# A prefix log-sum-exp kernel: TensorE's unrolled products become a loop in a loop, and semaphores are set by hand

## The chip, the cores and the metric

The kernel runs on one core of one Trainium2 chip. The metric is the device time of one execution in microseconds (us), as the median of several runs. Lower is better.

## The reference

For each of 4 batches, a running log-sum-exp is taken along 4096 rows, separately in each of 4128 columns. Input and output are float32, 270.5 MB each.

```python
B, S, D = (4, 4096, 4128)
out[:, 0, :] = x[:, 0, :]
for t in range(1, S):
    mx = np.maximum(out[:, t - 1, :], x[:, t, :])
    out[:, t, :] = mx + np.log(np.exp(out[:, t - 1, :] - mx) + np.exp(x[:, t, :] - mx))
```

## The kernel before

The fast path `_fast` computes log(prefix sum of exp(x)). It also gathers a few sums and lowest values into a flag. If the flag says that the plain exponentials were out of range, a slow path `_general` does the work again; with this input it is not taken.

**Tiles.** The work is cut into 44 steps, 11 for each batch. A step holds 384 rows (`R` = 3: each of 128 partitions holds three consecutive rows), or 256 rows in one step of each batch (the first of batch 0, the last of the others). A step is loaded by one DMA of 6192 KB (4128 KB for the short ones) and stored by one DMA of the same size from the same tile `xt`. There are `BUFS` = 4 such tiles in turn. SyncE issues all loads and stores in an order written out by hand: the store of step k when its four logarithms are done, then the load of step k + 3, which goes into the tile of step k - 1 and waits until the store of that step has landed.

**Chunks.** The 4128 columns of a step are worked on in four chunks: three of 1024 columns, with a running base `base0` to `base2` in PSUM, and one of 1056, whose base is in `carry` in SBUF. For each chunk ScalarE takes the exponential (L115), VectorE adds up the rows inside each partition (`sums`, L119), TensorE multiplies with the triangle `excl` to get what lies in the partitions above (`head`, L126; `head_rest`, L134 and L136, for the last chunk, 512 columns at a time through `q`), VectorE adds this base to the rows (`add`, L150; `add_rest`, L143; `keep`, L155, for the last chunk), TensorE passes the last row on with `pick` (`pass_on`, L159), and ScalarE takes the logarithm (L171). GpSimd copies the first row of each batch for the flag (L197), and VectorE reduces these copies and the last bases (L202, L166).

**Order.** Each engine has a list of steps, in an order given by the tables `ORDER`, `DORDER`, `PORDER` and some for the first and last steps. A loop emits from the lists whatever has its needs met, and the framework sets the semaphores between engines from the tiles that each instruction reads and writes. All engines are fully unrolled; on TensorE, all 781 products stand one after another in the program. A float32 product shows as two weight loads and two matmuls in the trace.

Of the kernel before, what the change touches and what calls it, by code (L numbers as in the profile page):

```python
# [6 lines left out]

# [5 lines left out]
P = 128  # L13
# [10 lines left out]
SPLIT = False  # L24
# [5 lines left out]
def _constants(nc, pool):  # L30

    def triangle(base, name):
        t = pool.tile([P, P], FP32, name=name)
        nc.gpsimd.memset(t, 1.0)
        nc.gpsimd.affine_select(
            out=t, in_=t, pattern=[[1, P]], compare_op=ALU.is_ge,
            fill=0.0, base=base, channel_multiplier=-1,
        )
        return t

    excl = triangle(-1, "excl")
    pick = pool.tile([P, P], FP32, name="pick")
    nc.gpsimd.memset(pick, 0.0)
    nc.gpsimd.affine_select(
        out=pick, in_=pick, pattern=[[0, P]], compare_op=ALU.not_equal,
        fill=1.0, base=-(P - 1), channel_multiplier=1,
    )
    ones = pool.tile([P, 1], FP32, name="ones")
    nc.gpsimd.memset(ones, 1.0)
    return excl, pick, ones  # L50


def _fast(ctx, tc, x, out, flag):

# [9 lines left out]
    excl, pick, ones = _constants(nc, consts)  # L64
    xpool = ctx.enter_context(tc.tile_pool(name="xpool", bufs=BUFS))
    cpool = ctx.enter_context(tc.tile_pool(name="cpool", bufs=1))
    pkeep = ctx.enter_context(tc.tile_pool(name="pkeep", bufs=1, space=bass.MemoryType.PSUM))
    prest = ctx.enter_context(tc.tile_pool(name="prest", bufs=2, space=bass.MemoryType.PSUM))

    carry = cpool.tile([P, rest], FP32, name="carry")  # L70
    first = cpool.tile([1, D], mybir.dt.bfloat16, name="first")
    low = cpool.tile([1, 1], FP32, name="low")
    part = cpool.tile([P, 5 * B], FP32, name="part")
    every = cpool.tile([P, 1], FP32, name="every")
    nc.vector.memset(carry, 0.0)  # L75
    nc.vector.memset(part, 0.0)
    base = [pkeep.tile([P, CH], FP32, name=f"base{c}") for c in range(3)]

    ctx.enter_context(tc.manual_schedule())

    class Step:
        def __init__(self, b, row, r):
            self.b, self.row, self.r = b, row, r
            self.first = row == 0
            self.last = row + P * r == S

# [4 lines left out]
        def load(self):  # L91
            full = xpool.tile([P, R, D], FP32, name="xt")
            self.xt = full[:, :self.r, :]
            nc.sync.dma_start(out=self.xt, in_=self.dram(x))

        def store(self, lo=0, hi=D):
            nc.sync.dma_start(out=self.dram(out)[:, :, lo:hi], in_=self.xt[:, :, lo:hi])

    class Chunk:
        def __init__(self, step, c):  # L100
            self.t, self.c = step, c
            self.a = c * CH
            self.w = CH if c < 3 else rest
            self.end = c == 3
            self.q = {}
# [7 lines left out]
        def exp(self):  # L113
            rows = self.rows(0, self.t.r)
            nc.scalar.activation(rows, rows, ACT.Exp)  # L115

        def sums(self):
            for j in range(1, self.t.r):
                nc.vector.tensor_tensor(  # L119
                    out=self.row(j), in0=self.row(j - 1), in1=self.row(j), op=ALU.add)  # L120

        def head(self):
            t = self.t
            own = self.row(t.r - 1)
            for s in range(0, CH, MM):
                nc.tensor.matmul(base[self.c][:, s:s + MM], lhsT=excl, rhs=own[:, s:s + MM],  # L126
                                 start=t.first, stop=True, skip_group_check=True)

        def head_rest(self, i):
            t = self.t  # L130
            s, w = subs[i]
            q = self.q[i] = prest.tile([P, MM], FP32, name="q")
            if not t.first:
                nc.tensor.matmul(q[:, :w], lhsT=pick, rhs=carry[:, s:s + w],  # L134
                                 start=True, stop=False, skip_group_check=True)
            nc.tensor.matmul(q[:, :w], lhsT=excl, rhs=self.row(t.r - 1)[:, s:s + w],  # L136
                             start=t.first, stop=True, skip_group_check=True)

        def add_rest(self, i):
            t = self.t  # L140
            s, w = subs[i]
            rows = t.xt[:, :, self.a + s:self.a + s + w]
            nc.vector.tensor_tensor(  # L143
                out=rows, in0=rows, in1=self.q[i][:, :w].unsqueeze(1).to_broadcast([P, t.r, w]),
                op=ALU.add)

        def add(self):
            t = self.t
            rows = self.rows(0, t.r)
            nc.vector.tensor_tensor(  # L150
# [3 lines left out]
        def keep(self):  # L154
            nc.vector.tensor_copy(carry[HI:P, :], self.row(self.t.r - 1)[HI:P])  # L155

        def pass_on(self):
            for s in range(0, CH, MM):
                nc.tensor.matmul(base[self.c][:, s:s + MM], lhsT=pick,  # L159
                                 rhs=self.row(self.t.r - 1)[:, s:s + MM],  # L160
                                 start=True, stop=False, skip_group_check=True)

        def total(self):
            own = carry if self.end else base[self.c]
            i = 4 * self.t.b + self.c
            nc.vector.tensor_reduce(  # L166
                out=part[HI:P, i:i + 1], in_=own[HI:P, :self.w], axis=AX.X, op=ALU.add)

        def ln(self):
            rows = self.rows(0, self.t.r)  # L170
            nc.scalar.activation(rows, rows, ACT.Ln)  # L171

    steps = []
    for b in range(B):
# [5 lines left out]
        for r in parts:  # L180
            steps.append(Step(b, row, r))
            row += P * r
# [3 lines left out]
    T = len(steps)  # L186
    heads = [k for k in range(T) if steps[k].first]
    done = set()
    act, dve, pe, pool, sync = [], [], [], [], []

    def put(queue, name, work, *needs):
        queue.append((name, work, needs))

    def lowest(t, c):

        a, w = c * CH, CH if c < 3 else rest
        nc.gpsimd.tensor_copy(first[:, a:a + w], t.xt[0:1, 0, a:a + w])  # L197

    def lower(t):

        i = 4 * B + t.b
        nc.vector.tensor_reduce(out=low, in_=first, axis=AX.X, op=ALU.min)  # L202
        nc.vector.tensor_scalar(
            out=part[0:1, i:i + 1], in0=low, scalar1=1.0 / LIMIT, scalar2=2 * LIMIT, op0=ALU.is_lt, op1=ALU.mult)

    for k, t in enumerate(steps):
        C = chunks[4 * k:4 * k + 4]
        prev = chunks[4 * k - 4:4 * k] if k else []
        W = len(subs)

        def exp(c):
            put(act, ("exp", k, c), C[c].exp, ("load", k))

        def ln(kk, c):
            put(act, ("ln", kk, c), chunks[4 * kk + c].ln, ("keep" if c == 3 else "pass", kk, c),
                *[("low", kk, c)] * steps[kk].first)

        order = {0: FIRST, T - 2: LATE, T - 1: LAST}.get(k, ORDER)
        for o in order:
            if o[0] == "e":  # L220
                exp(int(o[1]))
            elif o[0] == "n":
                put(act, ("exp", k + 1, int(o[1])), chunks[4 * k + 4 + int(o[1])].exp, ("load", k + 1))
# [4 lines left out]
        if t.first:  # L228
            for c in range(4):
                put(pool, ("low", k, c), lambda t=t, c=c: lowest(t, c), ("exp", k, c),  # L230
                    *[("lower", j) for j in heads if j < k])

        def sums(c):
            put(dve, ("sums", k, c), C[c].sums, ("exp", k, c))

        def add(c):
            put(dve, ("add", k, c), C[c].add, ("head", k, c))

        for o in DORDER:
            if o[0] == "s":  # L240
                sums(int(o[1]))
            elif o[0] == "a":
                add(int(o[1]))
            else:
                for i in range(W):
                    put(dve, ("rest", k, i), lambda i=i, C=C: C[3].add_rest(i), ("headr", k, i))
        put(dve, ("keep", k, 3), C[3].keep)
        for j in heads:
            if k == j + min(4, heads[1] - 1):
                put(dve, ("lower", j), lambda j=j: lower(steps[j]), *[("low", j, c) for c in range(4)])  # L250
        if t.last and k < T - 1:
            for c in range(4):
                put(dve, ("total", k, c), C[c].total, ("keep" if c == 3 else "pass", k, c))

        def head(c):
            put(pe, ("head", k, c), C[c].head, ("sums", k, c), ("total", k - 1, c) if k and steps[k - 1].last else ("sums", k, c))

        def headr(i):
            put(pe, ("headr", k, i), lambda C=C: C[3].head_rest(i), ("sums", k, 3),
                ("keep", k - 1, 3) if k else ("sums", k, 3), ("rest", k, i - 2) if i >= 2 else ("sums", k, 3))  # L260

        def onward(c):
            put(pe, ("pass", k, c), C[c].pass_on, ("add", k, c))

        for o in PORDER:
            if o[0] == "h":
                head(int(o[1]))
            elif o[0] == "p":
                onward(int(o[1]))
            else:  # L270
                headr(int(o[1]))

        if k < BUFS:
            put(sync, ("load", k), t.load)
    for c in range(4):
        if any(o == f"p{c}" for o in LAST) and not any(o == f"l{c}" for o in LAST):
            put(act, ("ln", T - 1, c), chunks[-4 + c].ln, ("keep" if c == 3 else "pass", T - 1, c))
    for k, t in enumerate(steps):
        if k < T - 1:
            put(sync, ("store", k), t.store, *[("ln", k, c) for c in range(4)])  # L280
# [112 lines left out]
```

## Time and profile before

| | |
|---|---|
| median of 3 runs | 1263.26 us (1262.83 to 1263.33) |
| profiled execution, own time | 1263.05 us |
| its span, first to last instruction | 1261.3 us |
| DMA moved | 541.40 MB, mean 429 GB/s |
| share of the span in which packets of the data queue (q1) were under way, over 16 DMA engines | 99.5% |
| busy: PE / DVE / ACT / POOL | 61% / 84% / 73% / 2% |
| instruction queues: q8 / q14 | 13 packets, 0.21 MB / 14 packets, 0.11 MB |

The span is measured inside the profiled execution; 1.75 us of its own time lie outside the span. PE is TensorE, DVE is VectorE, ACT is ScalarE, POOL is GpSimd, SP is SyncE, which issues the DMAs. "Share" is of the span. Queues q8 and q14 carry the program's instructions to the engines; they use the same 16 DMA engines as the data.

### The profile page before, as it was taken

How to read it: one execution, taken by the hardware profiler on the slowest of the kernel's cores; microseconds unless marked ns; L12 is line 12 of the kernel's file. 1: busy time of each engine (PE TensorE's matmuls, PEld its weight loads, DVE VectorE, ACT ScalarE, POOL GpSimd, SP SyncE). 2: the span in 40 equal slices, each digit the busy share in tenths (PEclk: the TensorE clock that was granted, in tenths of full speed). 3: DMA queues.
4: the chain of work that ended last, by engine and by line, in shares of the span. 5: the costliest groups of instructions: out<-in, count | busy, mean ns of one | idle time of the engine just before them, and what ended most of it. 6: DMA issues, size and time to landing. Idle time of an engine off the chain costs nothing.

```text
span 1261.3 us, 4886 instructions
## 1 busy us (share of the span) xinstructions
PE 767.4 (61%) x1562; PEld 308.9 (24%) x1562; DVE 1053.9 (84%) x672; ACT 925.6 (73%) x353; POOL 26.2 (2%) x25
## 2 busy tenths in 40 slices
PE   4667665565655556655566666665556666665564
PEld 1222222222222222222222222222222222222221
DVE  4999997889878898888789889888878988988785
ACT  4987777777777777768579767766866877766792
POOL 2000000000100000000010000000010000000000
PEclk9898888888888888888788888888877888888887
DMA  9999999999999999999999999999999999999998
GB/s 411 411 442 430 429 429 434 437 430 426 435 432 431 429 440 428 434 430 433 434 433 438 431 432 429 438 430 433 433 432 433 434 434 436 430 432 434 430 419 352
DMA packets 12699, 541.40 MB, mean 429 GB/s; under 512 B 1408, under 2 KB 1408, under 8 KB 1408
## 3 DMA queue, kind: packets, MB, share of 16 engines
q1 hardware_dynamic: 12672, 541.07, 99.5%
q8 instruction: 13, 0.21, 0.1%
q14 instruction: 14, 0.11, 0.0%
HBM read 270.53 MB, written 270.53 MB: 429 GB/s over the span
## 4 chain that ended last, share of the span: by engine, by line
DMA 55%; DVE 22%; ACT 12%; issue 5%; PE 5%; ACTq 0%; SPq 0%; DVEq 0%
DMA xt<-in_x_dram 31%; DMA out_dram<-xt 24%; DVE xt L150 10%; ACT xt L171 6%; DVE xt L119 6%; ACT xt L115 6%; PE base L126 4%; DVE xt L143 3%; DVE part L166 1%; PE base L159 1%; DVE carry L155 1%; DVE low L202 0%; PE q L136 0%; PE q L134 0%; ACTq L171 0%
## 5 line engine op out<-in xcount | busy, mean ns | idle before, releaser
L115 ACT ACTIVATE xt<-xt 128x3072 f32<-128x3072 f32 (+3 forms) x176 | 465.4, 2692 | 187.3 <-DMA xt<-in_x_dram 187.3
L126 PE MATMUL base<-xt,excl 128*128 128x512 f32 x528 | 348.4, 813 | 364.1 <-DVE xt L119 324.7
L171 ACT ACTIVATE xt<-xt 128x3072 f32<-128x3072 f32 (+3 forms) x176 | 470.1, 2695 | 133.4 <-PE base L159 133.1
L119 DVE TENSOR_TENSOR xt<-xt 128x1024 f32<-128x1024 f32 (+1 forms) x336 | 417.4, 1246 | 129.9 <-ACT xt L115 124.0
L150 DVE TENSOR_TENSOR xt<-xt,base 128x3072 f32<-128x3072 f32 (+1 forms) x132 | 429.3, 3252 | 56.8 <-PE base L126 56.8
L159 PE MATMUL base<-xt,pick 128*128 128x512 f32 x528 | 260.9, 617 | 110.6 <-DVE xt L150 110.6
L126 PEld LDWEIGHTS base<-xt,excl 128*128 128x128 f32 x528 | 131.7, 265 | 546.2 <-issue 467.4
L159 PEld LDWEIGHTS base<-xt,pick 128*128 128x128 f32 x528 | 90.2, 189 | 282.1 <-DVE xt L150 216.9
L143 DVE TENSOR_TENSOR xt<-xt,q 128x1536 f32<-128x1536 f32 (+1 forms) x132 | 153.6, 1214 | 6.1 <-PE q L136 6.0
L136 PE MATMUL q<-xt,excl 128*128 128x512 f32 (+1 forms) x264 | 106.2, 486 | 1.7 <-DVE xt L119 1.7
L134 PE MATMUL q<-carry,pick 128*128 128x512 f32 (+1 forms) x240 | 93.9, 473 | 0.0
L134 PEld LDWEIGHTS q<-carry,pick 128*128 128x128 f32 x240 | 44.5, 189 | 58.5 <-issue 30.1
L136 PEld LDWEIGHTS q<-xt,excl 128*128 128x128 f32 x264 | 45.6, 190 | 47.9 <-issue 46.4
L197 POOL CAST first<-xt 1x1024 bf16<-1x1024 f32 (+1 forms) x16 | 25.1, 1574 | 927.0 <-ACT xt L115 927.0
L155 DVE COPY carry<-xt 32x1056 f32<-32x1056 f32 x44 | 31.1, 706 | 1.5
L202 DVE TENSOR_REDUCE low<-first 1x1 f32<-1x4128 bf16 x4 | 17.8, 4440 | 0.1
L166 DVE TENSOR_REDUCE part<-base 32x1 f32<-32x1024 f32 x12 | 14.1, 1223 | 0.1
L166 DVE TENSOR_REDUCE part<-carry 32x1 f32<-32x1056 f32 x4 | 5.0, 1238 | 0.0
L311 PE MATMUL q<-ones,every 128*1 128x1 f32 x2 | 0.2, 163 | 6.1 <-DVE every L309 6.1
L354 ACT ACT_TABLE_LOAD x1 | 1.3, 1283 | 0.8 <-PEq L377 0.8
L75 DVE MEMSET carry<- 128x1056 f32 x1 | 0.9, 938 | 1.1 <-PEq L377 1.1
L311 PEld LDWEIGHTS q<-ones,every 128*1 128x1 f32 x2 | 0.1, 80 | 6.1 <-issue 6.1
(13 smaller groups left out, 2.5 us busy)
## 6 DMA issues: line engine op xcount, KB each, us to landing
xt<-in_x_dram SPq DMA_DIRECT2D x40, 6192.0 KB, 43.8
out_dram<-xt SPq DMA_DIRECT2D x40, 6192.0 KB, 33.0
xt<-in_x_dram SPq DMA_DIRECT2D x4, 4128.0 KB, 31.7
out_dram<-xt SPq DMA_DIRECT2D x4, 4128.0 KB, 29.5
```

Source lines behind the costliest of these rows:

```text
L115: nc.scalar.activation(rows, rows, ACT.Exp)
L119: nc.vector.tensor_tensor(out=self.row(j), in0=self.row(j - 1), in1=self.row(j), op=ALU.add)
L126: nc.tensor.matmul(base[self.c][:, s:s + MM], lhsT=excl, rhs=own[:, s:s + MM], start=t.first, stop=True, skip_group_check=True)
L134: nc.tensor.matmul(q[:, :w], lhsT=pick, rhs=carry[:, s:s + w], start=True, stop=False, skip_group_check=True)
L136: nc.tensor.matmul(q[:, :w], lhsT=excl, rhs=self.row(t.r - 1)[:, s:s + w], start=t.first, stop=True, skip_group_check=True)
L143: nc.vector.tensor_tensor(out=rows, in0=rows, in1=self.q[i][:, :w].unsqueeze(1).to_broadcast([P, t.r, w]), op=ALU.add)
L150: nc.vector.tensor_tensor(out=rows, in0=rows, in1=base[self.c].unsqueeze(1).to_broadcast([P, t.r, CH]), op=ALU.add)
L155: nc.vector.tensor_copy(carry[HI:P, :], self.row(self.t.r - 1)[HI:P])
L159: nc.tensor.matmul(base[self.c][:, s:s + MM], lhsT=pick, rhs=self.row(self.t.r - 1)[:, s:s + MM], start=True, stop=False, skip_group_check ...
L166: nc.vector.tensor_reduce(out=part[HI:P, i:i + 1], in_=own[HI:P, :self.w], axis=AX.X, op=ALU.add)
L171: nc.scalar.activation(rows, rows, ACT.Ln)
L197: nc.gpsimd.tensor_copy(first[:, a:a + w], t.xt[0:1, 0, a:a + w])
```

## The change

TensorE's products are no longer unrolled. An outer loop runs over the batches and an inner loop over the steps of a batch; the first step of a batch stands in the outer loop by itself, because its products start new sums. The tile of a step is reached through a register, which holds the byte offset of one of four slots in a single SBUF tensor `xs`. A step of 256 rows now lies at the end of its slot, so that its last row is where that of the others is. The loop is placed so that its first instruction is the first of a block of instructions that is fetched together (`head_slot`).

Because the framework cannot follow tiles through such a register, all waits are written by hand, in one critical section for all engines. VectorE raises a semaphore `turn` after each group of sums, each `add` and the first `add_rest`; TensorE waits until it is at least 1 and takes 1 off, before eight of its nine groups of products of a step. The other engines count on one semaphore each, and each of the four slots has one semaphore for its loads and one for its stores. The other engines stay unrolled, and the orders of all engines, the tile sizes, the operations and the DMAs are those of before. In the built program ScalarE has 410 instructions and waits in place of 607, VectorE 733 in place of 783, SyncE 269 in place of 241; TensorE has 34 products in place of 781.

```diff
-        def head(c):
-            put(pe, ("head", k, c), C[c].head, ("sums", k, c), ("total", k - 1, c) if k and steps[k - 1].last else ("sums", k, c))
...
+AWAITED = {"h0", "h1", "p0", "h2", "p1", "r0", "p2", "r2"}
...
+class Line:
...
+    def wait(self, sem, value):
+        if self.seen.get(sem.num, 0) < value:
+            self.engine.wait_ge(sem, value)
+            self.seen[sem.num] = value
...
+    raw = consts.tile([P, 4 * BUFS * R * D], mybir.dt.uint8, name="xs")
+    xs = raw.bitcast(FP32).rearrange("p (s j d) -> p s j d", s=BUFS, j=R)
...
+            self.xt = xs[:, k % BUFS, R - r:R, :]
...
         def sums(self):
             for j in range(1, self.t.r):
-                nc.vector.tensor_tensor(
+                if j > 1:
+                    dve.ended += 1
+                    end.then_inc(dve.sem, 1)
+                    dve.wait(dve.sem, dve.ended)
+                end = nc.vector.tensor_tensor(
                     out=self.row(j), in0=self.row(j - 1), in1=self.row(j), op=ALU.add)
...
+    def emit(line):
+        for name, work, needs in line.steps:
+            for sem, value in sorted({ends[n] for n in needs}, key=lambda e: e[1]):
+                line.wait(sem, value)
+            end = work()
+            if line is sync:
+                sem = (landed if name[0] == "load" else stored)[name[1] % BUFS]
+                ends[name] = (sem, 16 * (name[1] // BUFS + 1))
+                end.then_inc(sem, 16)
+            elif name[0] in turns or name[0] == "rest" and name[2] == 0:
+                end.then_inc(sems["turn"], 1)
+            else:
+                line.ended += 1
+                ends[name] = (line.sem, line.ended)
+                end.then_inc(line.sem, 1)
...
+    def product(o, t, new):
+        c = int(o[1])
+        def own(a, w):
+            return raw[:, bass.ds(t + 4 * ((R - 1) * D + a), 4 * w)].bitcast(FP32)
...
+        if o in AWAITED:
+            nc.tensor.sem_inc(sems["turn"], -1).wait_op(sems["turn"], 1, "sem-ge")
+        for ps, lhsT, rhs, start, stop in work:
+            end = nc.tensor.matmul(ps, lhsT=lhsT, rhs=rhs, start=start, stop=stop, skip_group_check=True)
+        end.then_inc(sems["pe"], 1)
+
+    def tile_of(t, new):
+        slot = nc.tensor.snap((t % BUFS) * (4 * R * D))
         for o in PORDER:
-            if o[0] == "h":
-                head(int(o[1]))
-            elif o[0] == "p":
-                onward(int(o[1]))
-            else:
-                headr(int(o[1]))
...
+            product(o, slot, new)
+
+    with tc.tile_critical():
+        _constants(nc, pool, excl, pick, ones)
+        nc.tensor.wait_ge(pool.sem, pool.ended)
...
+        emit(dve)
+        emit(act)
+        emit(pool)
+        emit(sync)
+        pe = mybir.EngineType.PE
+        with nc.Fori(0, T, N, engines=OrderedEngineSet([pe]), head_slot={pe: 0}) as b:
+            tile_of(b, True)
+            with nc.tensor.Fori(b + 1, b + N) as t:
+                tile_of(t, False)
...
     good = nc.values_load(flag, min_val=0, max_val=1, skip_runtime_bounds_check_because="a comparison gives 0 or 1")
...
+    with tc.tile_critical():
+        for sem, value in stored:
+            nc.sync.wait_ge(sem, value)
```

The diff is cut to its core; the last three lines stand at the very end of the kernel.

## The prediction

> **What bounds the kernel now.** I read the page first: the shares, the row of DMA, the queues.
>
> ```profile
> span 1261.3 us, 4886 instructions
> PE 767.4 (61%) x1562; PEld 308.9 (24%) x1562; DVE 1053.9 (84%) x672; ACT 925.6 (73%) x353; POOL 26.2 (2%) x25
> ...
> DMA  9999999999999999999999999999999999999998
> ...
> q1 hardware_dynamic: 12672, 541.07, 99.5%
> q8 instruction: 13, 0.21, 0.1%
> q14 instruction: 14, 0.11, 0.0%
> ```
>
> No engine is full, and DMA is, in every slice but the last. A packet of 49536 bytes takes 1.829 us on its DMA engine, one of 33024 takes 1.222 us, and each of the 16 engines carries 640 and 64 of them: 640 x 1.829 + 64 x 1.222 = 1248.8 us. The span is only 12.5 us longer. So the question is what these 12.5 us are, and next whether compute can come back as the bound. For that I read the chain where it is bound by compute, early on:
>
> ```profile
> 30.02 2.76 ACT xt L115
> ...
> 55.59 2.75 ACT xt L115
> ...
> 80.97 2.75 ACT xt L115
> ...
> 105.94 2.75 ACT xt L115
> ```
>
> With tiles loaded ahead, a step of compute takes 25.4 us (55.59 to 80.97). Its DMA takes 16 x 1.829 = 29.3 us. Compute has 3.9 us to spare in each step. Then the end, as windows (the last two columns are the share of DMA and GB/s) and by SyncE's waits:
>
> ```profile
> 1182.00:1214.00 32.00, 19.23 (x38) 7.78 (x39) 25.77 (x17) 23.52 (x10) 0.00 (x0) 0.84 1.00 432
> 1214.00:1230.00 16.00, 11.33 (x28) 4.82 (x27) 14.55 (x11) 16.00 (x8) 0.00 (x0) 0.97 0.92 399
> 1230.00:1245.00 15.00, 13.62 (x32) 5.96 (x31) 12.70 (x10) 6.72 (x4) 0.00 (x0) 0.92 0.95 407
> 1245.00:1262.00 17.00, 0.19 (x2) 0.11 (x2) 4.65 (x6) 2.05 (x2) 0.00 (x0) 0.53 0.68 291
> ```
>
> ```profile
> SPq L388 <- DMA out_dram<-xt: 7.9, 1, 7.9
> ```
>
> DMA is no longer full after 1214, which looks like an end bound by compute. The landings say otherwise. For each transfer the trace has the instants at which its 16 shares landed, one from each DMA engine. Shares of one transfer land 0.7 us apart at 12.6 us, 3.0 at 184, 5.3 at 404, 6.5 at 745 and 8.4 at 1228. The engines drift apart, and a step can start only when the last share has landed (the last load lands between 1188.7 and 1197.03, and ScalarE starts on it at 1197.05). At the end, most engines have stored step 42 at 1247.1 and wait for the last store, issued at 1247.08; they finish it by 1258.2. The latest engine ends step 42 at 1250.72, goes straight on, and 9.78 us later, at 1260.5, the last share lands. So **one late DMA engine, never idle, sets the time**, and compute has some 2.3 us to spare in the tail.
>
> Why is it late? Instruction packets go over the same engines. Matching landings from transfer to transfer, each of TensorE's 16 KB packets (q8, about 1.05 us) puts one engine 1.5 us back, nearly always another engine. Each 8 KB packet (q14, 0.31 us) costs some 0.8 us. Six of these come when VectorE has run another 128 or so instructions (87, 309, 516, 741, 964, 1172 us), and as far as they can be told apart they all fall on one engine: the latest. Its 8.3 us are 0.6 from the first load, 6 x 0.81 = 4.9 of VectorE's code and 2.8 of another kind: from 124 to 419 us, where most engines change from a load to a store at once, late ones take 0.3 to 0.9 us longer over a packet. This ends when the engines have drifted apart.
>
> **The change, part by part.**
>
> TensorE's code. Twelve of the thirteen q8 packets go. That is 12 x 1.5 = 18 us of lateness, but spread over engines that are not the latest. I see none of the twelve on the one that sets the time: 0 us. Bounds: -4 us if two or three of them did push it (the engines could not be told apart before 300 us), 0 if none.
>
> VectorE's and ScalarE's code. VectorE has 733 instructions in place of 783, and in a full step 15 in place of about 17. At 128 a packet, that is one packet in 8.3 steps, or five before the last load in place of six: -0.8 us on the latest engine. ScalarE's four packets become three, on an engine with little lateness: 0.
>
> The drift that is left. The spread that ended the slow changes from load to store came in part from TensorE's packets: four of them before 419 us, 6 us of some 33 in the sum over 16 engines. The slow changes add about 1.9 us to that sum in each step, so they go on for about three more steps, at 0.2 us a step on the latest engine: +0.5 us. Bounds: -2 (drift that does not come at all) and +6 (0.2 us for all the 30 remaining steps).
>
> The start. SyncE passes a no-operation and a waiting branch ahead of its first load. SyncE's nearest rows are the seven waits at the end of the kernel, 0.066 us apart: 2 x 0.066 = +0.13 us, bounds 0.05 and 0.4. All later DMA shifts with it.
>
> The end. After the last store has landed, SyncE has 13 more waits, branches and drains to pass than before: 13 x 0.066 = +0.86 us, bounds 0.4 and 1.5. Before, only 0.83 us lie between the last landing and the end of the span. Reading the flag and leaving the first critical section lie under the 7.9 us wait at L388: 0; without that cover, the 2 us from the flag (1250.06) to the wait (1252.1).
>
> TensorE's work in a step. Eight operations on `turn`, nine or so register additions and the loop's own few, about 20 instructions at 0.05 to 0.066 us, 1.0 to 1.3 us in a step. Where products are queued, they lie under the matmuls (a group of four takes 1.72 us). Where TensorE waits, they are exposed: ahead of the first `head` VectorE waits 1.24 us for it already, and each tenth there is a tenth of a step, against 3.9 us to spare. Queued behind a waiting TensorE are only its own later products, and `add` and the logarithms wait for those. The back edge lies between the last product of a step and the first `head` of the next, where TensorE idles 4.45 us. Cost: 0, as long as a step stays under 29.3 us and the tail takes less than 2.3 us more. VectorE's waits between two sums were there before (each second sum waited for the first); the loads, stores and their order are the same, and the slots change no size: 0.
>
> Against the loop speaks the Trainium skill, "Runtime: NRT & Kernel Launch", section "Instruction fetch mechanics": a taken branch whose target is outside the window of fetched pages stalls for a fetch. By that rule a loop longer than its window would fetch at each of 44 turns; this one, about 180 instructions counted as the trace counts them, starts at the head of a block, and one q8 packet carries about 250 (3300 records over 13), so by the rule it would cost nothing, and the sum would stay. No run here shows a taken back edge.
>
> Sum, against the profiled execution: 1263.05 + 0 - 0.8 + 0.5 + 0.13 + 0.86 = 1263.74 us. The median stands 0.21 us above that execution: 1264.0 us. A difference under about 0.2%, 2.5 us, is taken here as none.
>
> **The rivals.**
>
> Faster, as TensorE's packets do set the latest engine. For: they are two thirds of the instruction bytes, and the second and third latest engines, 7.0 us late, carry them. Against: the latest one jumps at VectorE's packets, four times by 0.8 to 1.0 us after 500 us. If its lateness falls from 8.3 to about 4, the time is 1264.0 - 4 = 1260.0 us. Chance 0.22.
>
> Slower, as the engines stay in step. If fewer fetches leave them nearly together, the slow change from load to store, which now ends after ten steps, lasts for all 44: half to all of the +6 us above, 1267 to 1270 us, say 1268. It decides from about 15 more such steps on. For: it stopped when the spread was above 5 us. Against: the slow changes spread the engines by themselves, and so end themselves. Chance 0.18.
>
> Slower, as each operation on `turn` lets TensorE run empty. The rows show 0.59 us for a matmul record, 0.43 us from one to the next, so a full stop could expose 0.16 to 0.6 us. Eight of them in the last step, which is one queue of products from 1227.56 to 1243.6, are 1.3 to 4.8 us; over the 2.3 us to spare that is up to +2.5: 1266.5 us. Chance 0.08.
>
> The change does not do what it says: the loop's code is fetched at every turn. 44 packets in place of 13 are 31 x 1.5 = 46 us over 16 engines, about +3 us on each: 1267 us, and a stall over 4.45 us at each turn would come on top. Against: the code is short and aligned. Chance 0.04.
>
> **How the numbers follow.** My case, no change that can be told, has 0.48, for 1262 to 1266.5. The range takes in most of the first two rivals: 1259.8 to 1268.5. Faster by over 0.2% (under 1260.7): 0.22. Slower by over 0.2% (over 1265.8): the three slower rivals, 0.30. Within: 0.48.
>
> **What would show it.** In the profile after: q8 falls from 13 packets to one or two, q14 to about 11. DMA stays at 9 in all slices, and the rate near 429 GB/s. The landings of the last load still spread over 6 to 9 us, with steps of 0.8 us about 240 us apart on the latest engine. SyncE's last wait ends some 1.7 us before the end of the span, not 0.8. The early step of compute takes 25.4 to 26.5 us. I am wrong if the last spread falls under 5 us (first rival), if slow packets at the changes from load to store go on past 700 us (second), or if matmul groups in the last step are more than 1.8 us apart (third).

## The result, and the profile after

The changed kernel takes 1266.34 us (median of 9 runs, 1265.83 to 1267.95), the kernel before 1263.1 us beside it (9 runs, 1262.54 to 1263.33): 3.2 us more, a ratio of 1.0028 (95% interval 1.0018 to 1.0038). The forecast was 1264.0 us, with a range of 1259.8 to 1268.5. The time lies in the range, but past the 2.5 us within which the likeliest case, no change, was to stay.

The page of the changed kernel, the rows that answer to those shown of before:

```profile
span 1264.1 us, 5372 instructions
...
PE 760.5 (60%) x1562; PEld 308.8 (24%) x1562; DVE 1054.9 (83%) x672; ACT 925.7 (73%) x353; POOL 23.9 (2%) x25
...
DMA  9999999999999999999999999999999999999997
...
q1 hardware_dynamic: 12672, 541.07, 99.3%
q14 instruction: 11, 0.09, 0.0%
q8 instruction: 1, 0.02, 0.0%
```

The engines do what they did; DMA is still at 9 in all slices but the last. TensorE's 13 packets of code (q8) are one. The q14 packets fell from 14 to 11 in the span; the trace has one more behind the span's end.

The loop costs TensorE little. Its timeline at the first `head` of step 2, which is the first turn of the inner loop to be reached over a back edge (the last columns: how long the engine stood idle before, and what ended that), first in the changed kernel:

```profile
62.63 2.07 PE L304 MATMUL base<-xs,excl 128*128 x2 [4.44 <-PEq L302]
```

and in the kernel before:

```profile
60.76 3.75 PE L126 MATMUL base<-xt,excl 128*128 128x512 f32 x4 [4.45 <-issue]
```

4.44 us idle against 4.45: the back edge lies inside the wait for VectorE's first sums. By the Trainium skill, "Runtime: NRT & Kernel Launch", section "Instruction fetch mechanics", a taken branch to code that is no longer held has to fetch it; one q8 packet in the whole run, ahead of the first product, says that this loop's code was held over its 44 turns, so here rule and trace agree. In the last step there is one small gap, ahead of the first `pass`:

```profile
1233.96 1.96 PE L304 MATMUL base<-xs,pick 128*128 x4 [0.16 <-PEq L302]
```

From there on the chain of waits of the changed kernel has the products queued without a gap:

```profile
1239.35 3.43 PE q L304 x8
1242.79 1.72 PE base L304 x4
1244.50 0.38 PE q L304 x4
```

A group of four `pass` products still takes 1.72 us, so the operations on `turn` do not let TensorE run empty there. From its first products to its last two the step takes 16.06 us (1228.42 to 1244.48) in place of 15.67 (1227.56 to 1243.23), 0.4 us more. And early on, with tiles loaded ahead, a step of compute takes 25.6 us (ScalarE's exponential that starts at 55.59 and 80.97 us before starts at 57.29 and 82.92 now) in place of 25.4; in the unrolled e1 below it is 25.4.

At the end, SyncE's last wait, and the windows over the tail (length, busy time and count of PE, PEld, DVE, ACT and POOL, granted clock, share of DMA, GB/s), both of the changed kernel:

```profile
SPq L426 <- DMA out_dram<-xs: 8.7, 1, 8.7
```

```profile
1214.00:1230.00 16.00, 11.11 (x27) 4.80 (x28) 15.09 (x10) 16.00 (x8) 0.00 (x0) 0.97 0.95 412
1230.00:1245.00 15.00, 14.71 (x34) 6.28 (x32) 11.52 (x8) 6.02 (x4) 0.00 (x0) 0.91 0.91 390
1245.00:1264.00 19.00, 0.19 (x2) 0.09 (x2) 5.84 (x8) 3.30 (x2) 0.00 (x0) 0.62 0.65 275
```

The shape is that of before: DMA falls below full after 1214, and one or two late engines carry the end (the two latest shares of the last load land 0.04 us apart). The last load's shares land from 1190.28 to 1197.58 (before: 1188.68 to 1197.03); the last share of the last store lands at 1262.35 us (1260.45), and the span ends 1.78 us later (0.89). The profiled execution's own time is 1266.34 us, 2.24 above its span (before 1.75).

So its 3.29 us over the profiled execution of before (1263.05) are: 0.22 at the first load (issued at 1.034 us, before 0.817), 0.33 more by the last load's last landing, 1.35 from there to the last landing, 0.89 from there to the end of the span, and 0.49 outside the span. The last two and the first, 1.6 us, are the same in nearly every kernel below that has the hand-set waits (but e8's end is 2.5 us longer than before and not 0.89, and e3 has 0.16 us more outside the span and not 0.49). The middle ones are DMA's. The 1.35 us are not the loop's: the unrolled form (e1, below) has them too, 64.76 us from the last load's last landing to the last landing, where the changed kernel has 64.77 and the kernel before 63.42. What is found at the start of the trace leads to the loop's part. A q8 packet, by its time the loop's own block, runs at 7.8 us, under the first load, and the engine that carries it lands its share at 14.59 us where the other 15 are done by 13.4. ScalarE's first work in the changed kernel:

```profile
14.62 7.36 ACT L133 ACTIVATE xs<-xs 128x2048 f32<-128x2048 f32 x4 [12.52 <-DMA xs<-in_x_dram]
```

Before it began at 13.29, 1.33 us earlier. Store 0 is issued at 40.99 us and not at 39.09, 1.90 us later; part of the rest, 0.6 us, is TensorE's later start in the first step (VectorE waits 2.18 us for the first `head`, before 1.97). Then, around 80 and 95 us, the queue turns from stores to loads and back, and in the changed kernel many packets are slow there at once: of those that start from 75 to 100 us, 24 of 208 take more than 0.2 us longer than usual, before 3 of 215. One window of each shows it (the last columns are again the share of DMA and GB/s), before:

```profile
85.00:100.00 15.00, 10.41 (x20) 4.04 (x21) 13.81 (x9) 12.26 (x5) 0.00 (x0) 0.89 1.03 443
```

and after:

```profile
85.00:100.00 15.00, 9.67 (x16) 3.58 (x16) 13.13 (x9) 13.88 (x6) 0.00 (x0) 0.77 1.02 416
```

The DMA engines are as busy (shares of 1.03 and 1.02) and move 6% fewer bytes. Where such a window is cut matters much (from 60 to 120 us it is 430 GB/s against 431), so the packets' own times decide. Summed over the data packets that start between 60 and 120 us, what each took beyond 1.829 us (1.222 for the smaller) is 0.19 us an engine before and 1.16 after. This figure, called the early excess below, is the clue that the experiments follow. Taken over all data packets of the span the same sum does not put the kernels in order (5.3 us an engine before, 6.0 after, 6.1 in e1, 5.0 in e5): it is the latest engine that counts.

### The profile page after: what moved, and what is told of

It is laid out like the page before. It is cut to its first block, busy times and chain, and to the rows that moved or that the text cites. A ratio compares the mean times of both kernels' runs of the same rounds, so it can differ in the third digit from the quotient of the medians.

```text
span 1264.1 us, 5372 instructions
## 1 busy us (share of the span) xinstructions
PE 760.5 (60%) x1562; PEld 308.8 (24%) x1562; DVE 1054.9 (83%) x672; ACT 925.7 (73%) x353; POOL 23.9 (2%) x25
## 5 line engine op out<-in xcount | busy, mean ns | idle before, releaser
L133 ACT ACTIVATE xs<-xs 128x3072 f32<-128x3072 f32 (+3 forms) x176 | 465.4, 2692 | 179.2 <-DMA xs<-in_x_dram 179.2
L171 ACT ACTIVATE xs<-xs 128x3072 f32<-128x3072 f32 (+3 forms) x176 | 470.2, 2695 | 142.5 <-PE base L304 142.5
L304 PE MATMUL base<-xs,excl 128*128 x528 | 345.0, 805 | 357.2 <-PEq L302 357.2
L141 DVE TENSOR_TENSOR xs<-xs 128x1024 f32<-128x1024 f32 (+1 forms) x336 | 418.5, 1250 | 117.9 <-ACT xs L133 112.0
L156 DVE TENSOR_TENSOR xs<-xs,base 128x3072 f32<-128x3072 f32 (+1 forms) x132 | 429.3, 3252 | 68.7 <-PE base L304 68.7
L304 PE MATMUL base<-xs,pick 128*128 x528 | 254.5, 604 | 106.7 <-PEq L302 106.7
L304 PEld LDWEIGHTS base<-xs,excl 128*128 128x128 f32 x528 | 129.8, 262 | 538.3 <-issue 537.9
L149 DVE TENSOR_TENSOR xs<-xs,q 128x1536 f32<-128x1536 f32 (+1 forms) x132 | 153.6, 1214 | 6.2 <-PE q L304 6.2
L304 PEld LDWEIGHTS base<-xs,pick 128*128 128x128 f32 x528 | 93.1, 189 | 262.3 <-issue 258.9
L304 PE MATMUL q<-xs,excl 128*128 x264 | 106.4, 487 | 1.9 <-PEq L302 1.9
L304 PEld LDWEIGHTS q<-xs,excl 128*128 128x128 f32 x264 | 46.6, 190 | 47.4 <-issue 47.4
```

The costliest lines, as they stand in the source:

```text
L133: return nc.scalar.activation(rows, rows, ACT.Exp)
L141: end = nc.vector.tensor_tensor(out=self.row(j), in0=self.row(j - 1), in1=self.row(j), op=ALU.add)
L149: return nc.vector.tensor_tensor(out=rows, in0=rows, in1=qs[i % 2][:, :w].unsqueeze(1).to_broadcast([P, t.r, w]), op=ALU.add)
L156: return nc.vector.tensor_tensor(out=rows, in0=rows, in1=base[self.c].unsqueeze(1).to_broadcast([P, t.r, CH]), op=ALU.add)
L171: return nc.scalar.activation(rows, rows, ACT.Ln)
L304: end = nc.tensor.matmul(ps, lhsT=lhsT, rhs=rhs, start=start, stop=stop, skip_group_check=True)
```

## The experiments

The theory after the comparison: some 1.6 us come from the hand-set waits (start, end, outside the span), and the rest from the loop by way of DMA. The rivals were that the sections themselves cost it, or that VectorE's code does. All eight kernels ran in 5 rounds beside the kernel before. The table collects them; "over before" is against the median of before on the same chip (1262.97, 1263.16 and 1262.9 us in the three sets, 1263.1 for the changed kernel).

| kernel | time us | over before | interval of the ratio | store 0 issued | early excess |
|---|---|---|---|---|---|
| before | 1263.1 | 0 | | 39.09 | 0.19 |
| after | 1266.34 | +3.2 | 1.0018 to 1.0038 | 40.99 | 1.16 |
| e1, unrolled | 1264.76 | +1.8 | 1.0005 to 1.0023 | 39.39 | 0.36 |
| e2, pad VectorE | 1268.15 | +5.2 | 1.0025 to 1.0052 | 40.82 | 1.75 |
| e3, pad GpSimd | 1266.2 | +3.2 | 1.0015 to 1.0034 | 40.97 | 1.93 |
| e4, two empty sections | 1263.0 | 0.0 | 0.9991 to 1.0009 | 39.12 | 0.36 |
| e5, loop not aligned | 1265.66 | +2.5 | 1.0011 to 1.0029 | 39.62 | 0.21 |
| e6, unrolled, late VectorE | 1266.44 | +3.3 | 1.0016 to 1.0035 | 42.01 | 1.95 |
| e7, before, late VectorE | 1263.97 | +1.1 | 1.0000 to 1.0018 | 40.72 | 1.63 |
| e8, one section | 1266.79 | +3.9 | 1.0020 to 1.0043 | 40.73 | 1.49 |

The intervals of neighbouring changed kernels overlap, so a difference of some 0.7 us between two of them (e5 and the changed kernel, say) is likely but not clear of noise by these intervals alone.

**e1: the change without the loop.** TensorE's products written out, with fixed slots; all waits as in the changed kernel.

```
-        with nc.Fori(0, T, N, engines=OrderedEngineSet([pe]), head_slot={pe: 0}) as b:
-            tile_of(b, True)
-            with nc.tensor.Fori(b + 1, b + N) as t:
-                tile_of(t, False)
+        for t in range(T):
+            tile_of(t, t % N == 0)
```

> The changed kernel with TensorE's two loops written out again (all waits by hand as before); nothing else differs. If the time is set by the one DMA engine that VectorE's instruction packets fall on, TensorE's 13 or 14 packets come back on other engines and the time stays within 1.2 us of the changed kernel (1265 to 1267.5 us), with the latest share of the last load again some 7 us behind the first. If all instruction packets count alike, it is slower than the changed kernel by 13 x 1.5 / 16 = 1.2 us to 4 us. If the missing packets had left the engines in step and so made the kernel slower, it is faster by 1 to 3 us (1263 to 1265). If the loop itself held TensorE up (1 to 2 us in the tail), it is faster by as much and the last store is issued earlier than 1248.4 us.

Measured: 1264.76 us, 1.79 us over before, where the changed kernel is 3.24 us over it, 1.45 more. TensorE's code is fetched as before:

```profile
q8 instruction: 13, 0.21, 0.1%
```

The change splits into halves of about one size: hand-set waits (with all else that is not the loop) 1.8 us, loop 1.5 us. The first half has the 0.22 us at the start, 1.78 us from the last landing to the end and 2.23 us outside the span: 0.22 + 0.89 + 0.48 = 1.59 us. The second half is not a price of TensorE's packets: there are twelve more of them here, in the faster of the two. But the time lies where two of the expectations had it, that the missing packets leave the engines in step, or that the loop holds TensorE up. The last store is indeed issued 1.0 us earlier (1247.40 against 1248.39), but the last load has by then landed 1.19 us earlier (1196.39 against 1197.58), so the loop's cost comes ahead of the tail, from DMA. e5 to e7 look for how.

**e2 and e3: more code on VectorE, on GpSimd.** Fifteen memsets of one element (9 ns apart) in each of 40 steps, in the changed kernel, on the one engine or on the other.

```
+        if 0 < k < T - 3:
+            def fill(k=k):
+                for i in range(PAD):
+                    end = nc.vector.memset(pad[:, i:i + 1], 0.0)
+                return end
+            dve.put(("pad", k), fill, *[("pad", k - 1)] * (k > 1))
```

> The changed kernel with 15 one-element memsets more on VectorE in each of 40 steps (none in the first and the last three), which fill a scratch tile that nobody reads. VectorE's code nearly doubles: some 4.7 more 8 KB packets. VectorE has 25.4 + 1 us of work against 29.3 us of DMA in a step, so the memsets by themselves cost nothing. If VectorE's packets fall on one engine, which is the latest, the time grows by 4.7 x 0.8 = 3.8 us (1269 to 1271 us) and the last load's shares spread over some 11 us. If packets count by their bytes over all engines, it grows by 4.7 x 0.8 / 16 = 0.2 us and the spread stays near 7 us. If VectorE's time counts in each step, it grows by up to 40 us.

> The changed kernel with the same 600 one-element memsets on GpSimd, paced by the last exponential of each step. As many more 8 KB packets as in the kernel with the memsets on VectorE. If each processor's packets fall on an engine of its own, and GpSimd's is not the latest, the time stays within 1 us of the changed kernel (1265.3 to 1267.3 us). If packets count whoever fetches them, it grows as much as with the memsets on VectorE.

The page of e2:

```profile
span 1266.0 us, 5972 instructions
...
q14 instruction: 15, 0.12, 0.0%
```

VectorE has ten packets of code ahead of the last load in place of five, and the last load's last share lands at 1200.59 us, 3.0 us later than in the changed kernel, 9.72 us behind the first share; the time rises by 1.9 us (5.18 - 3.24). GpSimd's five extra packets of the same size leave the time at +3.2 and the last load at 1197.91. So it is not the bytes of code that count, but whose code it is: 3.0 us for five packets, on the latest share, fit only if VectorE's packets go over one DMA engine, and it is the latest one (the trace does not name the engines). The time stays under the 1269 to 1271 us expected: a packet of VectorE's costs 1.9 / 5 = 0.4 us of the kernel's time, 0.6 us at the last load; the larger price, which the prediction used, held for the landing from one transfer to the next.

**e4: two empty critical sections in the kernel before.**

```
+    with tc.tile_critical():
+        pass
```

(ahead of the work and behind it)

> The kernel of before with two empty critical sections, one ahead of the first load and one at the very end; nothing else. It has what the changed kernel adds at both ends and nothing of its loop. If the fixed costs are as read from the rows of the changed kernel (first load 0.22 us later; about 0.9 us more after the last landing; some 0.45 us more outside the span), it is 0.9 to 1.6 us slower than before: 1264.0 to 1264.8 us. If these waits are hidden, it stays at 1263.1.

Measured: 1263.0 us, no change; the first load is issued at 0.923 us (+0.1) and the span ends 0.89 us behind the last landing, as before. The expectation was wrong: a section by itself costs nothing. What is left is the waits on the stores in it, which put the section's exit behind the last landing: SyncE has six records behind it here and before, and 17 in the changed kernel.

**e5: the loop without its alignment.**

```
-        with nc.Fori(0, T, N, engines=OrderedEngineSet([pe]), head_slot={pe: 0}) as b:
+        with nc.Fori(0, T, N, engines=OrderedEngineSet([pe])) as b:
```

> The changed kernel, with TensorE's loop no longer set at the head of a block of instructions (head_slot is left out). In the changed kernel one q8 packet runs at 7.8 us, under the first load; it puts one DMA engine 1.2 us back, so that the last share of that load lands at 14.59 us and not at 13.4, and ScalarE starts at 14.62 us. Theory A: this packet is what the loop costs (1.6 us between the unrolled form, 1264.8, and the loop, 1266.3). Then, if the packet goes or moves behind the first load, the load lands near 13.4 us, the slow packets at the changes of direction at 80 and 95 us fall from 1.2 us an engine to about 0.4, and the time is 1264.6 to 1265. Theory B: the loop costs because TensorE's other eleven packets are missing and the engines stay in step; then the time stays at 1266 to 1266.6 whatever the early packet does. Theory C: without the alignment the loop lies across two blocks and its code is fetched at each turn: some 44 or 88 q8 packets, and 1270 us or more.

The first load now has no packet of code under it (the one q8 packet runs at 1258.4 us), its last share lands at 13.47 us, and ScalarE begins so:

```profile
13.49 7.36 ACT L133 ACTIVATE xs<-xs 128x2048 f32<-128x2048 f32 x4 [11.39 <-DMA xs<-in_x_dram]
```

The window at the turns has its rate back:

```profile
85.00:100.00 15.00, 9.33 (x17) 3.43 (x17) 13.36 (x9) 13.15 (x5) 0.00 (x0) 0.89 1.01 436
```

The early excess is 0.21 us. The time is 1265.66 us: 0.7 us nearer to before, where theory A had 1.3 to 1.7. Theory C is out: no packet of TensorE's code runs during the 44 turns. Theory A has only about half of the loop's 1.5 us, and theory B is out as the whole of it, since the time fell. The other 0.7 us between e5 and e1 (+2.5 against +1.8) are open. The lack of TensorE's packets can still be their reason, and so can the 0.2 us that the loop adds to each early step: by them store 1 is issued 0.7 us later than in e1 (64.46 against 63.80) and store 4 1.4 us later (141.16 against 139.74), and no run takes them away. The last load's last share lands 0.73 us later in e5, of which 0.57 are there at 158 us already, but single profiles of like code differ that much: in e4 this landing is 0.77 us ahead of before.

**e6: the unrolled form, with compute started late.** Three memsets on VectorE ahead of the first sum of step 0.

```
+        if k == 0:
+            def late():
+                for w in (rest, 640):
+                    dve.wait(dve.sem, dve.ended)
+                    dve.ended += 1
+                    nc.vector.memset(carry[:, :w], 0.0).then_inc(dve.sem, 1)
+                dve.wait(dve.sem, dve.ended)
+                return nc.vector.memset(pad, 0.0)
+            dve.put(("late", k), late, ("exp", 0, 0))
```

> The unrolled form of the changed kernel (1264.8 us), with VectorE held up once, by some 1.7 us, before the first sum of step 0: three memsets of a tile (0.94, about 0.6 and 0.06 us), and nothing else. No instruction packet is added and none is moved by more than that. Theory A, second half: it is the later start of compute (store 0 issued at 41 us in place of 39.4) that lays the changes of direction at 80 and 95 us so that most engines pass them together, and this costs the latest engine 1 to 1.5 us. Then the time rises to 1265.8 to 1266.5, and the mean excess per engine between 60 and 120 us from 0.4 to above 1 us. Theory B: only the DMA engine that the packet hit matters, or the missing packets; then the delay is hidden behind DMA and the time stays at 1264.5 to 1265.1.

Measured: 1266.44 us, as theory A had it, 1.5 us more over before than e1 (+3.3 against +1.8), and an early excess of 1.95 us against 0.36. Store 0 is issued 2.6 us later than in e1, at 42.01; the loop's delay was 1.6 us, so the two do not cost alike microsecond by microsecond. DMA had the loads issued at the start to go on with, no code packet came or went (13 of q8, 11 of q14), and compute has 3.9 us to spare in every step; still a cost as large as the loop's is there, without a loop.

**e7: the same delay in the kernel before.**

```
+            if self is chunks[0]:
+                nc.vector.tensor_copy(carry[:, :CH], self.row(0))
+                nc.vector.memset(carry, 0.0)
```

> The kernel before, with VectorE held up once, ahead of the first sum of step 0, by a copy of 1024 columns and a memset of 1056 (about 0.7 and 0.94 us); nothing of the change is in it. Theory A: the start of compute sets how many engines pass the changes of direction at 80 and 95 us together, in whatever kernel, and a start 1.6 us later costs what it cost in the unrolled form (1264.8 to 1266.4): the mean excess per engine from 60 to 120 us rises from 0.19 us to more than 1, and the time from 1263.1 to 1264.3 to 1265. Theory B: it matters only together with the hand-set waits and VectorE's other packets; then the time stays at 1262.8 to 1263.4, because DMA is full and compute has 3.9 us to spare in each step.

The delay in VectorE's timeline:

```profile
14.93 0.70 DVE L119 COPY carry<-xt 128x1024 f32<-128x1024 f32 x1 [12.86 <-ACT xt L115]
15.91 0.94 DVE L120 MEMSET carry<- 128x1056 f32 x1 [0.29 <-DVE carry L119]
```

and the window at the turns:

```profile
85.00:100.00 15.00, 9.48 (x17) 3.51 (x18) 14.04 (x10) 13.76 (x6) 0.00 (x0) 0.89 1.03 410
```

410 GB/s in place of 443, and an early excess of 1.63 us in place of 0.19. The time is 1263.97 us, 1.1 us over before; the interval of the ratio ends at 1.0000, so the size is loose (0 to 2.3 us) and just below what was expected. The excess does not stay whole: the last share is 2.4 us later than before at 160 us and 0.6 us later at the last load, perhaps because engines that were thrown apart early pass later turns at different times.

The latest engine can be followed in all of these. The last share of the transfer that landed at 112.7 us before lands 2.80 us later in the changed kernel, 2.84 in e6 and 2.24 in e7, but 0.05 in e1 and 0.43 in e5. At the last load 0.55, 0.71, 0.65, -0.64 and 0.09 are left. So the loss is made by 112 us and in part won back; between the changed kernel and e1 1.2 us of it remain.

**e8: the waits on the last stores in the first section.**

```
         nc.vector.tensor_scalar(out=flag, in0=qs[0][:1, :1], scalar1=LIMIT, scalar2=None, op0=ALU.is_le)
+        last = [ends[("store", k)] for k in range(T - BUFS, T)]
+        for sem, value in last:
+            nc.sync.wait_ge(sem, value)
...
-    with tc.tile_critical():
-        for sem, value in stored:
-            nc.sync.wait_ge(sem, value)
```

> The changed kernel, with SyncE's waits on the last four stores at the end of the first critical section and no second section for them. The flag is then read behind the last landing and no longer under SyncE's wait of 8.7 us; one leaving of a section is gone. Theory A (the end costs what stands behind the last landing, instruction by instruction): reading the flag, the branches and the waits, about 2 us, come to lie behind the last landing, and 0.5 to 0.9 us of the second section go: the span ends 2.6 to 3.3 us behind the last landing in place of 1.78, and the time is 1267.2 to 1268. Theory B: the exit from a section is the larger part, and one less pays for the flag: 1266 to 1266.6. In both the packet of 8 KB that now runs after the end of the span should run before it, as the code behind it begins earlier than the last landing or not: I take it to stay behind.

SyncE's waits of e8 (in all, times, longest):

```profile
SPq L346 <- DMA out_dram<-xs: 12.6, 2, 9.7
...
SPq L394 <- SPq L394: 0.5, 1, 0.5
```

The wait for the last store is now L346, and the flag's read (L394) stands behind it. From the last landing to the end of the span it takes 3.39 us in place of 1.78: 1.6 us more. Yet the time rises by 0.65 us only (3.89 - 3.24), to between the ranges of the two theories. The rest came back in the last store: two of the three q14 packets at the end (1256.4 and 1256.9 us in the changed kernel, under the last store) run at 1263.9 us here, when the store is done, and the late engine takes 9.74 us for its eight packets of it (8 x 1.222 = 9.78), where in the changed kernel it took 10.42. So 0.7 us of the changed kernel's end seem to go with code for the way out, fetched while everyone waits for the last store. This need not be the change's own: the kernel before took 9.73 us there in its profile, but e4, which is the same with two empty sections, 10.44, as e1 did (10.45).

No version beat the kernel before, and none of the runs points to one: each gain found here (one packet of VectorE's code, no code under the first load) is smaller than the 1.6 us of the hand-set waits.

## Why the prediction was right or wrong

**What bounds the kernel** was read rightly. One late DMA engine sets the time: VectorE's five extra packets moved the last load by 3.0 us and the time by 1.9, and GpSimd's moved them by 0.3 and -0.1.

**TensorE's code: 0 us, right.** Its packets went from 13 to one, and the time did not fall; e1, which keeps them all, is not slower than the loop but faster. The first rival, 4 us faster, is out.

**VectorE's code: -0.8 us, half of it.** Five packets in place of six came as forecast. By e2 a packet is worth 0.4 us of time, so the term should have been -0.4.

**The drift that is left: +0.5 us; this is the step that failed.** The loop cost about 1.5 us. The prediction asked which packets would be missing, and let the lack of them prolong the slow changes by three steps. The slow changes did not go on: from 200 us to the last load the slow packets add up to 2.2 us an engine, before to 2.6. They came early and hard, at the turns around 80 and 95 us. About half of the cost goes back to an event of the start, which the prediction had not priced: it counted the loop's one packet and never asked under which transfer it would run. That packet, ahead of the first step, makes one share of the first load 1.2 us late and with it all of compute in the first steps. Without a loop, a start made late on purpose cost 1.5 us (e6) and 1.1 us (e7), against the loop's 1.5; taking the packet out of the first load gave 0.7 us back (e5). In all ten profiles the early excess is 0.2 to 0.4 us where store 0 was issued by 39.6 us, and 1.2 to 1.95 where it was issued after 40.7. The second rival, engines that stay in step for all steps, had the right place of loss and the wrong duration. That the time lies in the range is so in part luck: the range reached up to 1268.5 us for a rival that did not come about as described. The signs of being wrong looked elsewhere, and none of them came: the last load's shares still spread over 7.3 us, only four packets past 700 us take over 0.3 us longer than usual, and groups of products stay 1.72 us apart.

**The start: +0.13 us.** It measured 0.22.

**The end: +0.86 us, right** in its size (0.89; the 0.83 us that it read for the end before are also 0.89), and nearly in its reason. SyncE has 11 records more behind the last landing (17 in place of 6), where 13 were counted. e4's empty sections put none there and cost nothing. That the flag's read is hidden was right as well: uncovered, with one section less, it cost 1.6 us in the span (e8), where the prediction named 2 us for the flag alone.

**Outside the span: nothing was forecast, 0.49 us came.** An 8 KB packet of code runs at 1265.2 us, behind the span's end, in the changed kernel; before, the last three lay under the last store, at 1255 to 1257 us. In every kernel with the hand-set waits the time lies 1.91 to 2.24 us above the span, in the three without them 1.69 to 1.75. That the late packet causes this fits all of these, but no run moved it alone.

**TensorE's work in a step: 0, right for the steps that DMA bounds**, and so was the reason: the back edge lies in 4.44 us of idle time, and the 0.4 us more of the last step stay inside the time to spare. The third and the fourth rival are out. In the early steps, which compute bounds, 0.2 us a step were added. That is within the 25.4 to 26.5 us forecast for such a step, but the forecast took it to be free; as a late start turned out to cost time, this may not have been.

With the sizes that the runs gave, the sum is 1263.1 - 0.4 (VectorE's packet) + 1.6 (start, end, outside) + 1.5 (loop) = 1265.8 us; 0.5 us are left open, in the hand-set half (e1 is 1.8 us over before, where its terms give 1.2). The profiles place them behind the last load, in the 1.35 us more up to the last landing, 0.7 of which are the last store's on the late engine. That these belong to the change is not shown, since e4's profile has them too (64.80 us in place of 63.42) and its median did not rise. How the loop still costs 0.7 us when its packet does not lie under the first load is open too; the early steps are one possibility.

## What to carry to other kernels

Where DMA is full, a compute delay that every later step could absorb may still be paid: it moves the instants at which the queue turns between loads and stores, and with them how many packets are slow at a turn. So ask of an added or moved fetch of code not only how many there are, but over which DMA engine each goes and under which transfer it runs: here one packet under the first load seems to have cost 0.7 us, and the twelve that were saved gained nothing. And what must follow the last landing (a section's exit, a flag's read, code not yet fetched) is paid, however idle the engines are.

## What the runs showed that was not expected

Five extra packets of VectorE's code cost 1.9 us and five of GpSimd's nothing: VectorE's seem to go over one DMA engine, the latest, and GpSimd's not over that one. A start of compute 1.6 us later (e7) made 32 packets slow from 75 to 100 us in place of 3, and the rate from 85 to 100 us fell from 443 to 410 GB/s, with DMA busy throughout. The loop's 44 turns, aligned or not, fetched nothing: the only packet of TensorE's code ran ahead of the turns when the loop was aligned (at 7.8 us, under the first load), and behind them when it was not (at 1258.4 us, under the last store).
